# Attention scores of the first 128 tokens: one 32-bit matmul of 128 columns from plain queries and keys

## The chip, the core and the metric

The kernel runs on one core of one Trainium2 chip. Its time is the device time of one execution in microseconds (us); the time before is the median of three runs. Work runs on five engines, each with an instruction stream of its own: TensorE (PE in the profile; its weight loads are listed as PEld), VectorE (DVE), ScalarE (ACT), GpSimd (POOL) and SyncE (SP). They wait for each other through semaphores. TensorE writes to PSUM, eight banks of 128 x 512 32-bit numbers.

## The reference

One decoder layer over 512 tokens of width 1024, all in 32-bit floats. An input projection gives the parts of two mixers; a gated spatial mixer (A) and a sparse attention (B) are projected, gated and added, then follow an output projection and a feed-forward part. The attention, in the part that matters here:

```python
def block(i):                       # i = 0..3, blocks of 128 queries
    ...
    score = jnp.where(causal[None], score, -jnp.inf)
    sel_score, sel_idx = lax.top_k(score, top_k)       # top_k = 128
    valid = jnp.isfinite(sel_score)
    k_sel = gather(k, sel_idx).astype(jnp.float32)
    v_sel = gather(v, sel_idx).astype(jnp.float32)
    ...
    att = jnp.einsum('btgrd,btkgd->btgrk', qg.astype(jnp.float32), k_sel) * (HEAD_DIM ** -0.5)
    att = jnp.where(valid[:, :, None, None, :], att, NEG_INF)
    p = jax.nn.softmax(att, axis=-1)
    o = jnp.einsum('btgrk,btkgd->btgrd', p, v_sel).astype(q.dtype)
```

There are 8 query heads and 2 key heads, all of 128 dimensions. The first block has 128 causal keys at most and selects up to 128, so its queries attend to all their causal keys.

## The kernel before

**Split matmuls.** Most products take operands that are split into two parts of a reduced 32-bit type (`F32R`): hi is a copy in that type, lo is what is left. The helper `split` (line 359) makes hi with a ScalarE copy (line 360) and lo with a VectorE subtraction (line 361). `mm3` (line 51) then adds three matmuls into one PSUM tile: hi x hi (line 53), hi x lo (line 54) and lo x hi (line 55). Almost all matmuls of the kernel carry one of these three lines, so they are told apart by their tiles. Operands of the type `F32` go into a single `T.matmul` without a split; the token mixing of mixer A, `mix_mm` (line 914, matmul in line 918), is such a product.

**Order of work.** The order on each engine is that of the program text: the kernel is written out by hand, and the framework adds the waits between engines. Weights come through SP's queue into rotating buffers (`raw`), three of them. They are split ahead of use, hi by ScalarE (line 112) and lo by VectorE or GpSimd (line 116).

**Keys.** Early in the kernel, while the last queries are projected, `q_tasks` (line 800) runs small jobs ahead of each weight piece. Two of them are `k_b(0)` and `k_b(1)` (line 623): they split the rotated keys `kf` of one key head, 128 dimensions x 512 tokens, into `k_hi` and `k_lo`.

**Attention loop.** Line 1110 runs over 16 units of one block of 128 queries and one pair of heads (`aun`: block 3 first, block 0 last, four pairs each). Stage s issues: the value matmuls `at_pv` of unit s - 3; the scores `at_qk` (line 1013) of unit s; the sum with the mask and the row maximum, `at_soft_a` (VectorE, line 1033); the transposes `at_T` (line 1066) of unit s - 2 with their copies (ScalarE line 1123, VectorE line 1124); the normalization `at_soft_b` (line 1052) of unit s - 1; the exponential `at_exp` (ScalarE, line 1043) of unit s; the query split `at_split` (line 975) of unit s + 2; and a share of the gate projection as filler, `gb_part`. `at_qk` gives the queries to `mm3` as weights and the keys as the moving operand, for each of two heads. The number of columns is that of the causal keys, and at least 256.

**Buffers.** The rotated queries `qf` of two heads occupy the four buffers X0 to X3. Behind the loop these are taken over by the residual input, which the POOL queue loads again (`xr`, line 1138), each as soon as its buffer's last reader is done. The last reader of each is the unit of block 0 of that pair.

**Behind the loop.** The projection of mixer B (`W_PB`, the tiles `pb<-yb`) and then the output projection, which adds the residual.

Of the kernel before, what the change touches and what calls it, by code (L numbers as in the profile page):

```python
# [9 lines left out]
F32 = mybir.dt.float32  # L10
F32R = mybir.dt.float32r
I32 = mybir.dt.int32
AF = mybir.ActivationFunctionType
# [15 lines left out]
def block_kernel(ctx: ExitStack, tc: tile.TileContext, x, positions, w_ada, b_ada, w_in,  # L29
# [3 lines left out]
    T, V, A, P, SY = nc.tensor, nc.vector, nc.scalar, nc.gpsimd, nc.sync  # L33
# [8 lines left out]
    def bank(k, name="bank"):  # L42
        return psum.tile([128, 512], F32, name=name, tag=f"b{k}", bufs=1)

    def f(ap):
        return ap.bitcast(F32)
# [4 lines left out]
    def mm3(o, wl, rl, start, stop, **kw):  # L51
        (wh, wlo), (rh, rlo) = wl, rl
        T.matmul(o, wh, rh, start=start, stop=False, **kw)  # L53
        T.matmul(o, wh, rlo, start=False, stop=False, **kw)  # L54
        T.matmul(o, wlo, rh, start=False, stop=stop, **kw)  # L55
# [104 lines left out]
    mid = mid_stack.enter_context(tc.tile_pool(name="mid", bufs=1))  # L160
# [198 lines left out]
    def split(hi, lo, src):  # L359
        A.activation(hi, src, AF.Copy)  # L360
        V.tensor_sub(lo, src, f(hi))
# [217 lines left out]
    def rope_a(key, v, kind, m, t0=0):  # L579
        sh = t512("sh")[:m, t0:]  # L580
        V.stream_shuffle(sh, v, SW16 if kind == "q" else SW8)
        V.tensor_mul(sh, sh, tab[kind][:m, 1, t0:])
        V.tensor_mul(v, v, tab[kind][:m, 0, t0:])
        rp[key] = (v, sh)
# [6 lines left out]
    kf = mid.tile([128, 2, S], F32, name="kf", tag="A0", bufs=1)  # L591
# [3 lines left out]
    qf = [base.tile([128, 2, S], F32, name=f"qf{g}", tag=f"X{g}", bufs=1) for g in range(4)]  # L595
# [21 lines left out]
    k_hi = mid.tile([128, 2, S], F32R, name="k_hi", tag="k_hi", bufs=1)  # L617
    k_lo = mid.tile([128, 2, S], F32R, name="k_lo", tag="k_lo", bufs=1)

    def k_a(h):  # L620
        rope_a(("k", h), kf[:32, h], "q", 32)

    def k_b(h):
        split(k_hi[:, h], k_lo[:, h], kf[:, h])

    v_hi = mid.tile([128, 4, 256], F32R, name="v_hi", tag="v_hi", bufs=1)
    v_lo = mid.tile([128, 4, 256], F32R, name="v_lo", tag="v_lo", bufs=1)
# [157 lines left out]
    def q_rope(m):  # L785
        rope_a(("q", m), qf[m // 2][:32, m % 2], "q", 32)

    qstep = [0, 0]
    QT = {0: [lambda: q_rope(0), lambda: k_a(0)],
          1: [lambda: k_a(1), lambda: rope_b(("q", 0)), lambda: rope_b(("k", 0))],  # L790
          2: [lambda: rope_b(("k", 1)), lambda: qi_a(0)],
          3: [lambda: qi_b(0, 1), lambda: qi_a(1), lambda: qi_b(0, 0)],
          4: [lambda: qi_b(1, 1), lambda: qi_a(2), lambda: qi_b(1, 0)],
          5: [lambda: qi_b(2, 1), lambda: qi_a(3), lambda: qi_b(2, 0)],
          6: [lambda: qi_b(3, 1), lambda: qi_b(3, 0)],
          7: [ki_stats, lambda: k_b(0), ki_norm],
          8: [lambda: k_b(1)],
          10: [lambda: q_rope(1)]}

# [138 lines left out]
    def au_tasks():  # L938
        s = austep[0]
        austep[0] += 1  # L940
        if s == 0:
            for tk in range(4):
                ln_v(tk)
            rstd(rva, mva[:, :, 1], 4, 1.0)
            run_bg(0.8)
        elif s == 1:
            ln_v2(0)
            ln_v2(1)
        elif s == 2:
            ln_v2(2)  # L950
            ln_v2(3)
        for m in AT.get(s - 1, []):
            mix_ev(m)
        if s > 2:
            run_bg(1.6 if s < 8 else 2.0)
        if s in (20, 21):
            at_split(s - 20)
# [14 lines left out]
    AS = {}  # L972
    SCALE = 128 ** -0.5

    def at_split(u):
        i, hp = aun[u]
        qh = mid.tile([128, 2, 128], F32R, name="qh", tag="qh", bufs=2)
        ql = mid.tile([128, 2, 128], F32R, name="ql", tag="ql", bufs=2)
        split(qh, ql, qf[hp][:, :, i * 128:(i + 1) * 128])
        AS["q", u] = (qh, ql)  # L980
# [31 lines left out]
    yb = [(S2B[m // 2][:, m % 2], S2B[4 + m // 2][:, m % 2]) for m in range(8)]  # L1012
    def at_qk(u):
        i, hp = aun[u]
        nn = max((i + 1) * 128, 256)
        qh, ql = AS["q", u]
        g = hp // 2
        for e in range(2):
            p = bank(2 + e, "qk")
            mm3(p[:, :nn], (qh[:, e], ql[:, e]), (k_hi[:, g, :nn], k_lo[:, g, :nn]), True, True)  # L1020
            AS["s", u, e] = p

# [87 lines left out]
    for s in range(NU + 3):  # L1110
        if s >= 3:
            yh, yl, pp = at_pv(s - 3)
            A.activation(yh, pp, AF.Copy)
            V.tensor_sub(yl, pp, f(yh))
        if s < NU:
            at_qk(s)
            at_soft_a(s)
            if s == 0:
                pa_last[0]()
                at_split(2)  # L1120
        if 2 <= s <= NU + 1:
            for o, ol, p in at_T(s - 2):
                A.activation(o, p, AF.Copy)
                V.tensor_sub(ol, p, f(o))
        if 1 <= s <= NU:
            at_soft_b(s - 1)
        if s < NU:
            at_exp(s)
        if 0 < s < NU - 2:
            at_split(s + 2)  # L1130
        gb_part(GBN[s], 2 if s else 1)
# [495 lines left out]
    for q in range(-2, NQ):  # L1627
        g, u = 2 + q // 2, q % 2
# [282 lines left out]
```

## Time and profile before

| | |
|---|---|
| median of 3 runs | 824.95 us (824.74 to 825.56) |
| the profiled execution, its own time | 825.28 us |
| its span in the profile | 823.4 us |
| score matmuls in the span | 96, in 16 units of 6 |
| of these, block 0 | 24, in the units that start at 367.18, 371.83, 376.48 and 380.56 us |
| attention loop on TensorE | 306.8 to about 391.8 us |

The profile records one execution. A row of the timeline has the start in us from the start of the span, the duration in us, the engine, the line of the program, the operation, what it writes and reads (out<-in), its shape and how many are merged; in brackets stands how long the engine was idle before and what ended that. Matmuls overlap in the array, so a matmul's duration is longer than its share of TensorE's time, which is the distance from its start to the next one's. In rows of grouped instructions of one tile, three numbers behind the count are the shortest, median and longest duration in ns, and then come the first and last start. Waits are listed as who waited for whom, with us in total, times and the longest.

### The profile page before, as it was taken

The numbers are of one execution on the slowest core, as the hardware profiler recorded it, in microseconds if no ns is written. First come the engines' busy times: TensorE is split into PE (matmuls) and PEld (weight loads), VectorE is DVE, ScalarE is ACT, GpSimd is POOL, SyncE is SP. The second block draws the span as 40 slices with busy tenths as digits, with TensorE's granted clock in tenths as the row PEclk, the third lists the DMA queues.
The fourth block names the chain that finished last, engine by engine and source line by source line (L and its number), as shares of the span: only waits on it lengthen the run. The fifth ranks groups of instructions, "written<-read, shape, count | busy, mean of one in ns | idle before, by whom it ended". The sixth has DMA issues, their size and how long they took to land.

```text
span 823.4 us, 12920 instructions
## 1 busy us (share of the span) xinstructions
PE 808.5 (98%) x4920; PEld 722.0 (88%) x4920; DVE 684.9 (83%) x1167; ACT 427.7 (52%) x760; POOL 156.5 (19%) x171
## 2 busy tenths in 40 slices
PE   7999999999999999999999999999999999999996
PEld 6889889988888888988888899999999999888785
DVE  7989788798899558887688879889989888798676
ACT  6674444323332226665636586555555556666543
POOL 3060031362354411000000010222212222000001
PEclk9999999999999999999999999999999999999998
DMA  9974352332346553046630504889988978766543
GB/s 293 311 211 119 103 179 78 107 100 91 112 136 199 185 174 102 26 153 209 198 132 12 194 27 138 200 263 244 288 221 237 213 220 185 226 203 205 180 128 128
DMA packets 107197, 138.46 MB, mean 168 GB/s; under 512 B 6480, under 2 KB 77136, under 8 KB 106976
## 3 DMA queue, kind: packets, MB, share of 16 engines
q1 hardware_dynamic: 96832, 109.76, 42.8%
q0 software_dynamic: 9584, 27.07, 14.1%
q8 instruction: 38, 0.62, 0.3%
q10 hardware_dynamic: 720, 0.82, 0.3%
q14 instruction: 23, 0.19, 0.1%
HBM read 135.26 MB, written 23.07 MB: 192 GB/s over the span
## 4 chain that ended last, share of the span: by engine, by line
PE 51%; DVE 19%; DMA 5%; ACT 2%; issue 2%; POOL 0%; POOLq 0%; ACTq 0%; DVEq 0%
PE R L53 6%; PE R L54 6%; PE R L55 6%; DMA mraw<-in_w_ada_dram 5%; PE pfo L55 3%; PE pfo L54 3%; PE pfo L53 3%; DVE acc L177 3%; DVE sco L717 2%; DVE m L713 2%; PE pb L53 2%; PE pb L55 2%; PE pb L54 2%; DVE lo L116 2%; PE po L54 2%
## 5 line engine op out<-in xcount | busy, mean ns | idle before, releaser
L112 ACT ACTIVATE hi<-raw 128x1024 fp32r<-128x1024 f32 (+2 forms) x103 | 107.0, 1040 | 106.0 <-PE pb L54 35.7
L116 DVE TENSOR_TENSOR lo<-raw,hi 128x1024 fp32r<-128x1024 f32 (+2 forms) x67 | 81.1, 1214 | 29.4 <-ACT hi L112 28.9
L116 POOL TENSOR_TENSOR lo<-raw,hi 128x1024 fp32r<-128x1024 f32 x29 | 73.0, 2521 | 128.1 <-ACT hi L112 122.4
L53 PE MATMUL pb<-h,hi 128*128 128x512 f32 (+1 forms) x192 | 74.6, 388 | 0.0
L55 PE MATMUL pb<-h,lo 128*128 128x512 f32 (+1 forms) x192 | 73.9, 385 | 0.0
L54 PE MATMUL pb<-h,hi 128*128 128x512 f32 (+1 forms) x192 | 73.9, 385 | 0.0
L54 PE MATMUL pfo<-lo,za 128*128 128x512 f32 (+1 forms) x146 | 56.4, 386 | 0.3 <-DVE lo L116 0.3
L55 PE MATMUL pfo<-hi,za 128*128 128x512 f32 (+1 forms) x146 | 56.2, 385 | 0.0
L53 PE MATMUL pfo<-hi,za 128*128 128x512 f32 (+1 forms) x146 | 56.2, 385 | 0.0
L177 DVE SCALAR_TENSOR_TENSOR acc<-mraw,cols,acc 128x512 f32<-128x512 f32 x49 | 39.8, 813 | 19.6 <-DMA mraw<-in_w_ada_dram 18.6
L1239 POOL TENSOR_TENSOR sm<-sm,mhalf 128x1 f32<-128x1 f32 x8 | 5.3, 660 | 216.9 <-DVE sm L1238 216.9
L53 PE MATMUL R<-tb,sx 128*128 128x256 f32 x160 | 45.3, 283 | 1.1 <-ACT R L1661 0.7
L54 PE MATMUL R<-tb,sx 128*128 128x256 f32 x160 | 45.1, 282 | 0.0
L55 PE MATMUL R<-tb,sx 128*128 128x256 f32 x160 | 45.0, 281 | 0.0
L55 PE MATMUL R<-tb,lo 128*128 128x256 f32 x160 | 44.8, 280 | 0.0
L53 PE MATMUL R<-tb,hi 128*128 128x256 f32 x160 | 44.8, 280 | 0.0
L54 PE MATMUL R<-tb,hi 128*128 128x256 f32 x160 | 44.6, 279 | 0.0
L55 PEld LDWEIGHTS pb<-h,lo 128*128 128x128 f32 x192 | 36.0, 188 | 7.3
L54 PEld LDWEIGHTS pb<-h,hi 128*128 128x128 f32 x192 | 36.0, 188 | 6.9
L53 PEld LDWEIGHTS pb<-h,hi 128*128 128x128 f32 x192 | 36.0, 188 | 6.9
L324 POOL COPY sm<-sm 128x1 f32<-128x1 f32 x30 | 18.9, 631 | 117.0 <-ACT sm L323 116.9
L54 PE MATMUL pav<-lo,h 128*128 128x256 f32 x128 | 35.8, 279 | 0.0
(377 smaller groups left out, 2675.4 us busy)
## 6 DMA issues: line engine op xcount, KB each, us to landing
raw<-in_w_ffn_in_dram SPq DMA_DIRECT2D x44, 512.0 KB, 5.8
raw<-in_w_in_dram SPq DMA_DIRECT2D x40, 512.0 KB, 3.8
wsum<-in_w_ffn_out_dram POOLq DMA_DIRECT2D x30, 512.0 KB, 7.0
mraw<-in_w_ada_dram SPq DMA_DIRECT2D x28, 512.0 KB, 4.1
raw<-wsum SPq DMA_DIRECT2D x20, 512.0 KB, 3.9
raw<-in_w_ffn_out_dram SPq DMA_DIRECT2D x18, 512.0 KB, 4.5
s<-in_w_ada_dram SPq DMA_DIRECT2D x30, 256.0 KB, 5.6
wsum<-wsum POOLq DMA_DIRECT2D x10, 512.0 KB, 5.9
```

The source lines that it names most:

```text
L53: T.matmul(o, wh, rh, start=start, stop=False, **kw)
L54: T.matmul(o, wh, rlo, start=False, stop=False, **kw)
L55: T.matmul(o, wlo, rh, start=False, stop=stop, **kw)
L112: A.activation(hi[:, :m], e["raw"][:, :m], AF.Copy)
L116: e["lo"].tensor_sub(lo[:, :m], e["raw"][:, :m], f(hi[:, :m]))
L177: V.scalar_tensor_tensor(o, w, cs[:, j:j + 1], o, op0=OP.mult, op1=OP.add)
L324: P.tensor_copy(t, t)
L713: V.max(m8s[i], sco[i])
L717: V.match_replace(out=sco[i], in_to_replace=m8s[i], in_values=sco[i], imm_value=TAKEN)
L1239: P.tensor_tensor(r2[:, tk:tk + 1], r2[:, tk:tk + 1], mhalf[:, :1], op=OP.pow)
```

## The change

The units of block 0 no longer split their queries. Each of their heads has one matmul of two `F32` operands: the plain queries `qf` as weights and, as the moving operand, a plain copy of the first 128 keys, `k_pl`. This copy is made by ScalarE behind the split of the keys, one instruction for each key head. The other blocks keep their matmuls; the least number of 256 columns applied to block 0 alone and is gone with it.

```diff
@@ -617,11 +617,14 @@
     k_hi = mid.tile([128, 2, S], F32R, name="k_hi", tag="k_hi", bufs=1)
     k_lo = mid.tile([128, 2, S], F32R, name="k_lo", tag="k_lo", bufs=1)
 
+    k_pl = mid.tile([128, 2, 128], F32, name="k_pl")
+
     def k_a(h):
         rope_a(("k", h), kf[:32, h], "q", 32)
 
     def k_b(h):
         split(k_hi[:, h], k_lo[:, h], kf[:, h])
+        A.activation(k_pl[:, h], kf[:, h, :128], AF.Copy)
...
@@ -974,6 +977,8 @@
 
     def at_split(u):
         i, hp = aun[u]
+        if i == 0:
+            return
         qh = mid.tile([128, 2, 128], F32R, name="qh", tag="qh", bufs=2)
...
@@ -1012,11 +1017,15 @@
     def at_qk(u):
         i, hp = aun[u]
-        nn = max((i + 1) * 128, 256)
-        qh, ql = AS["q", u]
+        nn = (i + 1) * 128
         g = hp // 2
         for e in range(2):
             p = bank(2 + e, "qk")
+            if i == 0:
+                T.matmul(p[:, :nn], qf[hp][:, e, :nn], k_pl[:, g], start=True, stop=True)
+                AS["s", u, e] = p
+                continue
+            qh, ql = AS["q", u]
             mm3(p[:, :nn], (qh[:, e], ql[:, e]), (k_hi[:, g, :nn], k_lo[:, g, :nn]), True, True)
             AS["s", u, e] = p
```

## The prediction

> **What bounds the kernel now.** I read the page first, then the waits of TensorE over the whole span, then the timeline around the instructions that the change touches. All times are from one execution: 825.28 us, of which the profile's span holds 823.4 us. The median of the three runs is 824.95 us, so the profiled execution lies 0.33 us above it. Differences are worked out in the profile, and then taken off the median.
>
> ```profile
> span 823.4 us, 12920 instructions
> ...
> PE 808.5 (98%) x4920; PEld 722.0 (88%) x4920; DVE 684.9 (83%) x1167; ACT 427.7 (52%) x760; POOL 156.5 (19%) x171
> ...
> PEclk9999999999999999999999999999999999999998
> ```
>
> TensorE (PE) is busy for 98% of the span, with the full clock granted in every slice but a piece of the last. A busy share is modelled, so it alone doesn't prove the bound. The waits of TensorE do more, in us in total, times, longest:
>
> ```profile
> PE warm L502 <- DMA cst<-in_consts_dram: 5.3, 1, 5.3
> PE R L53 <- ACT R L1661: 0.7, 1, 0.7
> ...
> PE pv L54 <- DVE tl L1124: 0.2, 1, 0.2
> ```
>
> After the first load, no wait of TensorE is longer than 0.7 us, and the only one inside attention is 0.2 us. So in the attention loop the end is set by what TensorE itself has to stream, and other engines matter only if they become late for it.
>
> **The score matmuls that go.** The change touches the last four units of the loop, those of token block 0 (i = 0). The timeline of TensorE (start, duration, instruction) for the first, the second and the last of the four:
>
> ```profile
> 367.18 0.28 PE L53 MATMUL qk<-k_hi,qh 128*128 128x256 f32 x1
> ...
> 367.89 0.60 PE L1066 MATMUL pT<-cst,pt 128*128 128x128 f32 x4
> ```
>
> ```profile
> 371.83 0.28 PE L53 MATMUL qk<-k_hi,qh 128*128 128x256 f32 x1
> 371.95 0.28 PE L54 MATMUL qk<-k_lo,qh 128*128 128x256 f32 x1
> ...
> 372.42 0.28 PE L55 MATMUL qk<-k_hi,ql 128*128 128x256 f32 x1
> 372.54 0.60 PE L1066 MATMUL pT<-cst,pt 128*128 128x128 f32 x4
> ```
>
> ```profile
> 380.56 0.28 PE L53 MATMUL qk<-k_hi,qh 128*128 128x256 f32 x1
> ...
> 381.26 0.38 PE L1066 MATMUL pT<-cst,pt 128*128 128x128 f32 x2
> ```
>
> The 0.28 is the latency of one; what counts is the distance between starts, 0.12 us (371.83 to 371.95). A unit has two heads of three such matmuls, and occupies TensorE from its first score matmul to the first transpose: 0.71, 0.71 and 0.70 us here. Four units are 2.83 us, or 24 matmuls of 0.118 us. The two transposes behind them are not changed.
>
> **The matmuls that come.** Eight plain 32-bit matmuls, weights 128x128 (the queries) and 128 moving columns (the keys). The kernel has the same form elsewhere: the token mixing of the gated branch, line 918, has a plain 32-bit 128x128 as weights and 128 plain columns moving.
>
> ```profile
> L918 PEld LDWEIGHTS mix<-wmT,vg x64: 187/192/192, 187.1 to 227.9; 128*128 128x128 f32 x64
> L918 PE MATMUL mix<-wmT,vg x64: 270/275/275, 187.4 to 228.0; 128*128 128x128 f32 x64
> ```
>
> ```profile
> 187.15 0.39 PE L55 MATMUL pb<-h,lo 128*128 128x512 f32 x1
> 187.38 1.05 PE L918 MATMUL mix<-wmT,vg 128*128 128x128 f32 x8
> 188.19 0.48 PE L53 MATMUL pb<-h,hi 128*128 128x512 f32 x1
> 188.50 0.39 PE L54 MATMUL pb<-h,hi 128*128 128x512 f32 x1
> ```
>
> The loop over m and n issues 8 x 4 = 32 matmuls, and the trace has 64 records: each plain matmul is two instructions, with two weight loads. Four matmuls are the eight records from 187.38 to 188.19. The split matmul behind them is 0.31 us from its successor (188.19 to 188.50), where its kind takes 0.23 (187.15 to 187.38); those 0.08 belong to the plain group's end. So four cost 0.81 + 0.08 = 0.89 us, one costs 0.222, one record 0.111. The step from split to plain work shows no cost of its own: the split matmul ahead keeps its 0.23. In the changed loop the new matmuls are followed by the transposes, which are 128-column 32-bit work too, and the step back to split work stays where it is now. Eight cost 8 x 0.222 = 1.78 us.
>
> The saving on TensorE is 2.83 - 1.78 = **1.05 us**. No record of exactly these operands exists. From below, a record could stream its 128 columns at the rate of the split form, half of 0.118 = 0.059 us: 16 x 0.059 = 0.94, saving 1.89. From above, its weight load could stand in the open: 0.19 + 0.111 = 0.30 each, 4.82 in all, a loss of 1.99. I take 0.111, since line 918 agrees in shape, type and weight load.
>
> A rule speaks against the change: the Trainium skill, "FP8 and Floating Point Precision", section "TensorE Precision Notes", says that true 32-bit work takes four passes through the array, where the split form has three matmuls; it gives no price of a pass at 128 columns. Line 918 agrees with that if a pass costs half a record, 0.222 / 4 = 0.056 us, and then the sum stays 1.05; at a split matmul's 0.118 a pass, the change would lose, as the third rival below does.
>
> **What else is removed.** Four splits of the queries, each one ScalarE copy and one VectorE subtraction:
>
> ```profile
> L360 ACT ACTIVATE qh<-qf x16: 398/404/418, 279.9 to 375.3; 128x256 fp32r<-128x256 f32 x16
> L361 DVE TENSOR_TENSOR ql<-qf,qh x16: 415/420/426, 291.0 to 375.7; 128x256 fp32r<-128x256 f32 x16
> ```
>
> ScalarE loses 4 x 0.404 = 1.6 us and VectorE 4 x 0.420 = 1.7 us, two units ahead of the use. TensorE waits for neither, so I count nothing; the loop's one wait, 0.2 us, is in an earlier unit. These cuts also keep the softmax in step with the faster units. A unit's scores are normalized (line 1052) a stage before its transposes, and its transposed remainders (line 1124) come ahead of the value matmuls:
>
> ```profile
> 374.35 0.68 DVE L1124 TENSOR_TENSOR tl<-pT,th 128x512 fp32r<-128x512 f32 x1
> ...
> 375.14 0.48 DVE L1052 TENSOR_SCALAR pt<-pt,mx 128x128 f32<-128x128 f32 x2
> ...
> 375.78 0.19 PEld L54 LDWEIGHTS pv<-tl,v_hi 128*128 128x128 f32 x1
> ...
> 377.19 0.38 PE L1066 MATMUL pT<-cst,pt 128*128 128x128 f32 x2
> ```
>
> Normalized at 375.62, transposed at 377.19: 1.6 us of slack. Remainders at 375.03, loaded as weights at 375.78: 0.75 us. A unit gets 0.26 us shorter (1.05 / 4), so both hold.
>
> **What is added outside the loop.** Two ScalarE copies of keys, 128x128, behind the two splits of the keys near 90 us. Nearest row: a ScalarE pass of that shape in the loop takes 0.394 us; so at most 0.8 us for both, at least half the 128x256 split's 0.404 each, 0.4. The place:
>
> ```profile
> L1043 ACT ACTIVATE pt<-pt,mx 128x128 f32<-128x128 f32 x8 | 3.1, 394 | 1.5 <-DVE mx L1035 1.5
> ```
>
> ```profile
> 90.12 0.72 ACT L360 ACTIVATE k_hi<-kf 128x512 fp32r<-128x512 f32 x1
> 90.64 1.13 ACT L112 ACTIVATE hi<-raw 128x1024 fp32r<-128x1024 f32 x1
> ...
> 91.59 0.70 ACT L360 ACTIVATE k_hi<-kf 128x512 fp32r<-128x512 f32 x1
> ...
> 92.50 1.41 DVE L652 TENSOR_TENSOR v_lo<-pv,v_hi 128x256 fp32r<-128x256 f32 x4
> ...
> 93.83 1.22 DVE L116 TENSOR_TENSOR lo<-raw,hi 128x1024 fp32r<-128x1024 f32 x1
> 94.13 1.06 ACT L112 ACTIVATE hi<-raw 128x1024 fp32r<-128x1024 f32 x1 [1.85 <-issue]
> ```
>
> The first copy pushes the weight split at 90.64 by up to 0.4 us, to end at 92.2 instead of 91.8. Its remainder on VectorE starts at 93.83, behind v_lo, so 1.6 us of VectorE work covers it. The second falls into the 1.85 us in which ScalarE is idle. Cost nothing; with that cover gone, up to 0.8 us. It can't gain.
>
> **What moves.** The buffers of the queries become those of the reloaded residual (xr, line 1138, on the POOL queue). Their last reader was the split; now it is the score matmul, two units later.
>
> ```profile
> 361.99 0.62 POOL L1138 DMA_DIRECT2D xr<-in_x_dram  x1 [37.35 <-DVE ql L361]
> ...
> 376.41 0.53 POOL L1138 DMA_DIRECT2D xr<-in_x_dram  x1 [4.69 <-DVE ql L361]
> ```
>
> ```profile
> xr<-in_x_dram POOLq DMA_DIRECT2D x4, 512.0 KB, 3.6
> ```
>
> The first goes out near 367.7 instead of 361.99, and the last near 380.4 instead of 376.41 (ends of the units' matmuls, less the gain): four loads some 4 to 6 us late. POOL issues nothing else in that stretch, and the residual is wanted only by the output projection. They now run beside the loads of the next stage's weights, of which the second piece is the nearer:
>
> ```profile
> 386.52 1.22 DVE L116 TENSOR_TENSOR lo<-raw,hi 128x1024 fp32r<-128x1024 f32 x1
> ```
>
> ```profile
> 391.83 0.39 PE L53 MATMUL pb<-yb,hi 128*128 128x512 f32 x1
> ```
>
> Its split ends at 387.74, and TensorE uses it behind 24 matmuls of the first, at 391.83 + 24 x 0.23 = 397.4: 9.6 us of slack. Cost nothing.
>
> **Sum.** 825.28 - 1.05 = 824.23 us in the profiled execution's terms, **823.9 us** against the median.
>
> **The rivals.**
> *Cheaper records or shorter late waits (faster).* With 0.059 us a record the time is 824.95 - 1.89 = 823.1. A shift of phase could also shorten the late wait on R (0.7 us), giving 824.95 - 1.05 - 0.7 = 823.2. Line 918 speaks against the first, its wait on ScalarE's own chain against the second.
> *The gain is absorbed.* TensorE arrives earlier and waits for the softmax or for a load: 824.95. Against it, the slacks of 0.75, 1.6 and 9.6 us; for it, that 0.75 is small.
> *Four instructions a matmul.* Were the new matmul four instructions of 0.118 us instead of the two of line 918, 8 x 4 x 0.118 - 2.83 = +0.95: 825.9, slower by less than can be told. Against it, the 64 records for 32 matmuls; for it, nothing in the trace. The four passes that the Trainium skill names (page and section above) would be read so.
> *Weight loads in the open (slower).* The queries' plain weights can't be loaded under the matmul ahead. It decides from 2.83 / 16 = 0.177 us a record; at 0.30 it is +1.99, 826.9. Line 918 loads in 0.192 and still has 0.111 a record.
> *The moved loads delay the next weights (slower).* It decides once a weight load is more than 9.6 us late; with all four ahead of it, 4 x 3.6 = 14.4, TensorE waits 4.8: 824.95 - 1.05 + 4.8 = 828.7.
>
> **How the numbers follow.** What a measurement can tell from no change is about 0.2%, 1.65 us: from 823.3 to 826.6. Forecast 56%, cheaper records or late waits 18%, absorbed 10%, four instructions 3%, open weight loads 8%, moved loads 5%. Faster by over 0.2% is the second, 18%; slower the last two, 13%; within it the other three, 69%. The range of 822.9 to 825.4 holds the forecast, the absorbed case and most of the faster one; it leaves out the slower ones, 16%, and a little of the faster.
>
> **What would show it.** Sixteen records of scores from plain queries in the last four units, each unit 0.44 us from first score matmul to first transpose instead of 0.71; twelve query splits instead of sixteen; two copies near 91 us with no new wait of TensorE; the residual's loads released by TensorE. I am wrong if the records stand 0.15 us apart or more, or if a new wait of TensorE appears between 367 and 400 us.

## The result and the profile after

| | before | after |
|---|---|---|
| median | 825.16 us (824.59 to 826.51, 22 runs) | 823.93 us (822.93 to 826.04, 22 runs) |
| profiled span | 823.4 us | 822.3 us |

The ratio is 0.9987, with a 95% interval of 0.9981 to 0.9993: faster by 0.13%, or 1.1 us (0.6 to 1.6). The forecast was 823.9, a gain of 1.05. That 823.9 and 823.93 agree so closely is luck: the forecast starts from the 824.95 us of three runs, where 22 runs gave 825.16.

The page of the changed kernel:

```profile
span 822.3 us, 12898 instructions
...
PE 807.8 (98%) x4912; PEld 721.2 (88%) x4912; DVE 683.2 (83%) x1163; ACT 427.6 (52%) x758; POOL 156.3 (19%) x171
```

Eight matmul records fewer (24 go, 16 come), four VectorE instructions fewer, and two ScalarE instructions fewer (four go, two come). The new matmuls and what is left of the query split, in the view of their tiles:

```profile
L1025 PEld LDWEIGHTS qk<-k_pl,qf x16: 188/192/192, 366.9 to 379.8; 128*128 128x128 f32 x16
L1025 PE MATMUL qk<-k_pl,qf x16: 272/275/275, 367.0 to 380.0; 128*128 128x128 f32 x16
```

```profile
L360 ACT ACTIVATE qh<-qf x12: 398/406/417, 279.8 to 356.0; 128x256 fp32r<-128x256 f32 x12
```

TensorE in the first and the last unit of block 0:

```profile
367.01 0.61 PE L1025 MATMUL qk<-k_pl,qf 128*128 128x128 f32 x4
367.45 0.60 PE L1075 MATMUL pT<-cst,pt 128*128 128x128 f32 x4
...
379.62 0.61 PE L1025 MATMUL qk<-k_pl,qf 128*128 128x128 f32 x4
380.07 0.38 PE L1075 MATMUL pT<-cst,pt 128*128 128x128 f32 x2
```

A unit takes 0.44 us from its first score matmul to its first transpose (367.01 to 367.45; 0.45 in the last unit), where it took 0.71. One measure serves for all kernels below, the **block-0 stretch**: from the first score matmul of the first of the four units to the first transpose in the last. It contains the filler work too, which is the same in all of them. Before, it is 381.26 - 367.18 = 14.08 us, and after, 380.07 - 367.01 = 13.06: 1.02 us less. The changed kernel enters the stretch 0.17 us earlier and leaves it 1.19 us earlier; its span is 1.1 us shorter. So in these two executions the saving comes from the stretch and arrives at the end.

The waits of TensorE over the span:

```profile
PE warm L502 <- DMA cst<-in_consts_dram: 4.9, 1, 4.9
PE pfo L54 <- DVE lo L116: 1.0, 3, 0.4
PE modS L475 <- DVE accw L177: 0.4, 1, 0.4
PE R L53 <- ACT R L1683: 0.3, 1, 0.3
PE pfo L55 <- DVE gs L1795: 0.3, 1, 0.3
```

There is no wait in the loop. Behind it, the 0.7 us wait on R is gone and the waits on split weights have grown from 0.3 to 1.0 us: in these two executions late waits have moved, and they cancel. The last experiments return to that.

The two copies of keys on ScalarE, with the weight split behind the first and its remainder on VectorE:

```profile
90.48 0.38 ACT L627 ACTIVATE k_pl<-kf 128x128 f32<-128x128 f32 x1
90.68 1.13 ACT L112 ACTIVATE hi<-raw 128x1024 fp32r<-128x1024 f32 x1
...
92.15 0.38 ACT L627 ACTIVATE k_pl<-kf 128x128 f32<-128x128 f32 x1
...
93.67 1.22 DVE L116 TENSOR_TENSOR lo<-raw,hi 128x1024 fp32r<-128x1024 f32 x1
```

All of this run is 0.16 us earlier here; against that, the split starts 0.2 us late (90.68 for 90.64) and its remainder not at all (93.67 for 93.83).

The loads of the residual, on POOL's queue and in the list of DMA issues (median time to landing at the end):

```profile
367.92 0.62 POOL L1147 DMA_DIRECT2D xr<-in_x_dram  x1 [43.46 <-PE qk L1025]
...
380.53 0.53 POOL L1147 DMA_DIRECT2D xr<-in_x_dram  x1 [3.29 <-PE pT L1075]
```

```profile
xr<-in_x_dram POOLq DMA_DIRECT2D x4, 512.0 KB, 6.2
```

They are released by TensorE now, 4 to 6 us later, and land in 6.2 us instead of 3.6.

### The profile page after: what moved, and what is told of

It reads as the page before. It is cut to its first block, busy times and chain, and to the rows that moved or that the text cites. A ratio compares the mean times of both kernels' runs of the same rounds, so it can differ in the third digit from the quotient of the medians.

```text
span 822.3 us, 12898 instructions
## 1 busy us (share of the span) xinstructions
PE 807.8 (98%) x4912; PEld 721.2 (88%) x4912; DVE 683.2 (83%) x1163; ACT 427.6 (52%) x758; POOL 156.3 (19%) x171
## 4 chain that ended last, share of the span: by engine, by line
PE 53%; DVE 17%; DMA 5%; ACT 2%; issue 2%; POOL 0%; POOLq 0%; DVEq 0%; ACTq 0%
PE R L53 8%; PE R L54 8%; PE R L55 8%; DMA mraw<-in_w_ada_dram 4%; DVE acc L177 3%; PE pfo L55 3%; PE pfo L54 3%; PE pfo L53 3%; DVE lo L116 2%; DVE sco L720 2%; DVE m L716 2%; PE pb L53 2%; PE pb L55 2%; PE pb L54 2%; PE po L54 2%
```

## The experiments

Times in the table are of runs beside the kernel before, on the same chip. Where only one run was timed, its time is beside one run of before; such pairs scatter by more than the effects here, and what counts in them is the profile. Of block 1's units, those of the kernel before are 15.83 us by the same measure.

| kernel | median, us | of before, us | ratio, 95% interval | block-0 stretch, us |
|---|---|---|---|---|
| the change again | 823.55 | 824.81 | 0.9982 (0.9973 to 0.9991) | 13.06 |
| splits kept | 824.35 | 824.81 | 0.9993 (0.9983 to 1.0004) | 13.06 |
| split form, 128 columns | 824.89 | 824.81 | 1.0001 (0.9992 to 1.0011) | 13.81 |
| plain form, 256 columns | 824.71 | 824.81 | 0.9999 (0.9991 to 1.0008) | 14.73 |
| copies of keys alone | 824.84 | 824.51 | 0.9997 (0.9987 to 1.0007) | 14.09 |
| block 1 plain too | 823.51 | 824.51 | 0.9986 (0.9977 to 0.9994) | 13.06 |
| residual loaded late | 824.25 | 824.51 | 0.9991 (0.9980 to 1.0003) | 13.06 |
| split form, 192 columns | 826.16 (one run) | 825.49 | | 13.86 |
| plain form, twice 64 columns | 825.47 (one run) | 825.49 | | 14.67 |
| before, once more | 824.36 (one run) | 825.49 | | 14.09 |
| half weights added | 827.19 (one run) | 824.65 | | not compared |

The stretch of the same loop repeats within 0.01 us (14.08, 14.09, 14.09 for the three kernels with the old one; 13.06 five times for those with the new one), while the 95% intervals of the times in the table are 1.4 to 1.9 us wide. So questions of 0.1 to 1 us are decided by the stretch.

**Is it TensorE's stream? The change again, and with the splits kept.** The first has no edit.

> The changed kernel as it is, beside the kernel before on the same chip. Theory (TensorE's stream in the attention loop sets the time): units of block 0 take 0.44 us from first score matmul to first transpose instead of 0.71, 1.03 us less in all, so about 824.0 against 825.1. Rival (late waits of TensorE between 600 and 820 us carry part of the difference): the late waits, 3.0 us in all in both profiles seen so far, come out shorter than before by 0.3 us or more in this profile too.

The stretch is 13.06 us again, and the time is about 1.5 us (0.7 to 2.2) under before. The late waits of TensorE came out shorter as well, by the 0.3 us or more that the rival asks for: 2.4 us for 3.0 (counted as told under the last experiment). So this run alone doesn't settle where the time was gained; the kernel before, once more, bears on it.

The second makes the four query splits of block 0 that nobody reads:

```diff
     def at_split(u):
         i, hp = aun[u]
-        if i == 0:
-            return
         qh = mid.tile([128, 2, 128], F32R, name="qh", tag="qh", bufs=2)
```

> The changed kernel that still makes the four query splits of block 0 on ScalarE and VectorE, which nobody reads. Theory (TensorE's stream alone): the time of the change, 824.0, units still 0.44 us. Rival (part of the gain is the 1.6 us of ScalarE and 1.7 us of VectorE that the change removes): between the change and before, 824.5 or more, and a wait of TensorE in the loop.

Its profile, the tile of the split queries, the waits behind the loop and two rows of TensorE's timeline:

```profile
L360 ACT ACTIVATE qh<-qf x16: 398/404/417, 280.2 to 374.7; 128x256 fp32r<-128x256 f32 x16
```

```profile
PE R L53 <- ACT R L1668: 0.9, 1, 0.9
```

```profile
366.91 0.61 PE L1023 MATMUL qk<-k_pl,qf 128*128 128x128 f32 x4
...
379.97 0.38 PE L1073 MATMUL pT<-cst,pt 128*128 128x128 f32 x2
```

All sixteen splits are there again, and the stretch is still 13.06 us, with no wait in the loop. Removing the splits is worth nothing there. The time lies between the change and before, as the rival said, but its interval holds both; the profile has a late wait on R of 0.9 us, which the kernel before shows in one of two profiles (0.7 us; below). The time alone can't tell; the stretch does.

**Type or columns? The split form with 128 columns.**

```diff
-        nn = max((i + 1) * 128, 256)
+        nn = (i + 1) * 128
```

> The kernel before, with block 0's split matmuls cut from 256 columns to 128; no plain operands. Theory (the plain form is what makes 128 columns pay): a split matmul of 128 columns costs no less than one of 256, 0.118 us, so the time is that of before or more; if it costs as much as a plain matmul of 128 columns, 0.222 us, the four units take 24 x 0.222 = 5.33 us instead of 2.83, +2.5 us. Rival (only the columns count): 24 x 0.059 = 1.42 us, so -1.4 us against before, better than the change.

```profile
366.85 0.22 PE L53 MATMUL qk<-k_hi,qh 128*128 128x128 f32 x1
366.91 0.27 PE L54 MATMUL qk<-k_lo,qh 128*128 128x128 f32 x1
367.02 0.28 PE L55 MATMUL qk<-k_hi,ql 128*128 128x128 f32 x1
...
367.47 0.62 PE L1066 MATMUL pT<-cst,pt 128*128 128x128 f32 x4
```

Neither expectation holds. Half the columns save 0.09 us a unit (0.62 for 0.71), and 0.27 in the stretch, since the first transpose of each unit is now followed after 0.13 us instead of 0.11. The row distances tell why: the first matmul of the unit is followed after 0.06 us, each later one after 0.11. The stream alone would allow 0.06. Something else holds the later ones at 0.11, about what a plain record of 128 columns takes.

**What holds them? The split form with 192 columns, the plain form in two halves, and half weights.** The first has `nn = max((i + 1) * 128, 192)`.

> The kernel before with block 0's split matmuls at 192 columns instead of 256 (the last 64 belong to keys that aren't used). At 128 columns a unit was only 0.06 us shorter than at 256, 0.108 us a record. Theory (no record with its own weight load comes in less than about 0.11 us, and more columns cost once they exceed that): 192 columns cost 0.108 to 0.112 us a record, so a unit takes 0.65 to 0.67 us instead of 0.71. Rival (under 256 columns the split type streams at half its rate): 192 columns cost 1.5 times the 0.108 of 128, 0.16 us, so a unit takes 0.97 us.

```profile
368.37 0.25 PE L53 MATMUL qk<-k_hi,qh 128*128 128x192 f32 x1
368.46 0.27 PE L54 MATMUL qk<-k_lo,qh 128*128 128x192 f32 x1
368.57 0.28 PE L55 MATMUL qk<-k_hi,ql 128*128 128x192 f32 x1
...
369.02 0.60 PE L1066 MATMUL pT<-cst,pt 128*128 128x128 f32 x4
```

0.65 us: 0.09 for the first, 0.11 for the others. There is no slower stream under 256 columns, but a least distance. (The unit of 128 columns was 0.09 us shorter than that of 256, and not 0.06 as the expectation has it.) The plain form has it too:

```diff
-                T.matmul(p[:, :nn], qf[hp][:, e, :nn], k_pl[:, g], start=True, stop=True)
+                for c in (0, 64):
+                    T.matmul(p[:, c:c + 64], qf[hp][:, e, :nn], k_pl[:, g, c:c + 64], start=True, stop=True)
```

> The changed kernel with each plain matmul cut into two of 64 columns: the same products, twice the records and weight loads. Theory (about 0.11 us is also the least that a plain record takes): 8 records a unit of 0.108 to 0.111, 0.86 to 0.89 us instead of 0.44, +1.7 us in the four units. Rival (a plain record costs its columns alone, with 256 columns at 0.219 and 128 at 0.111): 0.055 us a record, a unit 0.44 us as in the change.

```profile
366.74 1.00 PE L1026 MATMUL qk<-k_pl,qf 128*128 128x64 f32 x8
367.58 0.61 PE L1076 MATMUL pT<-cst,pt 128*128 128x128 f32 x4
```

Eight records in 0.84 us: behind the first, which is followed after 0.06, they stand 0.11 apart. But for the first, half the columns don't shorten them. The last of the three adds to the split form of 128 columns, in each unit, 12 matmuls with weights of 64 queries, whose results nobody reads:

```diff
-        nn = max((i + 1) * 128, 256)
+        nn = (i + 1) * 128
...
             mm3(p[:, :nn], (qh[:, e], ql[:, e]), (k_hi[:, g, :nn], k_lo[:, g, :nn]), True, True)
+            for r in (0, 64) if i == 0 else ():
+                mm3(p[:64, 128 + 2 * r:256 + 2 * r], (qh[:, e, r:r + 64], ql[:, e, r:r + 64]),
+                    (k_hi[:, g, :nn], k_lo[:, g, :nn]), True, True)
```

> The kernel before with block 0's split matmuls at 128 columns (a unit of 0.62 us), and with 12 more split matmuls in each unit whose results nobody reads: the same products with weights of 64 queries instead of 128, 128 columns each. Theory (the least of 0.11 us a record is the load of 128 weight columns): with half the weights a record takes its stream, 0.058 us, so a unit takes about 0.62 + 12 x 0.058 = 1.3 us. Rival (it is a fixed price of an instruction): 12 x 0.11, a unit of 1.9 to 1.95 us.

```profile
366.98 0.19 PEld L53 LDWEIGHTS qk<-k_hi,qh 128*128 128x128 f32 x1
367.10 0.22 PE L53 MATMUL qk<-k_hi,qh 128*128 128x128 f32 x1
367.10 0.19 PEld L54 LDWEIGHTS qk<-k_lo,qh 128*128 128x128 f32 x1
...
367.21 0.19 PEld L55 LDWEIGHTS qk<-k_hi,ql 128*128 128x128 f32 x1
...
367.32 0.14 PEld L53 LDWEIGHTS qk<-k_hi,qh 128*64 128x64 f32 x1
367.38 0.23 PE L53 MATMUL qk<-k_hi,qh 128*64 128x128 f32 x1
367.38 0.14 PEld L54 LDWEIGHTS qk<-k_lo,qh 128*64 128x64 f32 x1
...
368.44 0.62 PE L1069 MATMUL pT<-cst,pt 128*128 128x128 f32 x4
```

With 64 weight columns (128*64 in the rows) and the same 128 moving columns, matmuls follow each other after 0.06 us, and a unit takes 1.34 us: 0.62 + 12 x 0.06. It isn't a price of the instruction. The least distance is the weight load, as the rows of the loads (PEld) show: behind a load of 128 columns the next load starts 0.11 us later (367.10, 367.21, 367.32), behind one of 64 columns 0.06 (367.32, 367.38). So a load of 128 columns takes about 0.11 us, and one of 64 at most 0.06. The Trainium skill, "TensorE: Matmul & The Clock Gate", section "LDWEIGHTS (loading the stationary operand)", gives the number of weight columns divided by 1.2 in nanoseconds, an estimate of 107 for 128 and 53 for 64. The trace agrees in the distance between loads, 0.11 us and 0.06; the rows of the loads themselves last longer, 0.19 and 0.14.

**Where does the plain form stop paying? 256 columns, and block 1 too.** The first computes 256 columns from both heads' copies and uses the half that it needs:

```diff
-                T.matmul(p[:, :nn], qf[hp][:, e, :nn], k_pl[:, g], start=True, stop=True)
-                AS["s", u, e] = p
+                T.matmul(p[:, :256], qf[hp][:, e, :nn], k_pl.rearrange("p h n -> p (h n)"), start=True, stop=True)
+                AS["s", u, e] = p[:, g * 128:(g + 1) * 128]
```

> The changed kernel with 256 moving columns in block 0's plain matmuls (both key heads' copies side by side; the half that belongs to the other head is computed and not used). Theory (a plain record's cost is its stream of columns): two records of 0.222 us a matmul, 16 x 0.222 = 3.55 us for the four units, +1.77 against the change and +0.72 against before: about 825.8. Rival (its cost is the weight load, or a fixed price of an instruction): still 0.111 us a record, the time of the change, 824.0.

```profile
366.81 1.03 PE L1025 MATMUL qk<-k_pl,qf 128*128 128x256 f32 x4
367.67 0.60 PE L1075 MATMUL pT<-cst,pt 128*128 128x128 f32 x4
```

0.86 us a unit, 0.215 a record; the stretch is 0.65 us longer than before and 1.67 longer than in the change. So at 256 columns the stream is the bound, at 128 the stream and the weight load are about equal. The time, 0.9999 (0.9991 to 1.0008), allows from -0.7 to +0.7 us and so can't show the +0.65.

The other makes block 1 plain as well:

```diff
-    k_pl = mid.tile([128, 2, 128], F32, name="k_pl")
+    k_pl = mid.tile([128, 2, 256], F32, name="k_pl")
...
-        A.activation(k_pl[:, h], kf[:, h, :128], AF.Copy)
+        A.activation(k_pl[:, h], kf[:, h, :256], AF.Copy)
...
-    bst = mid.tile([128, 4, 24], F32, name="bst")
+    bst = mid.tile([128, 4, 24], F32, name="bst", tag="qh", bufs=2)
...
-        if i == 0:
+        if i <= 1:
             return
...
-            if i == 0:
-                T.matmul(p[:, :nn], qf[hp][:, e, :nn], k_pl[:, g], start=True, stop=True)
+            if i <= 1:
+                T.matmul(p[:, :nn], qf[hp][:, e, i * 128:nn], k_pl[:, g, :nn], start=True, stop=True)
```

> The changed kernel with plain scores for block 1 too (256 columns, which the split form doesn't pad); a small statistics tile shares a buffer to make room. Theory (a plain record costs its columns): block 1 has eight heads of two records of 0.222 us instead of three of 0.118, 8 x (0.444 - 0.354) = +0.72 us against the change: 824.7. Rival (saving records and splits pays whatever the columns): 16 records instead of 24 at 0.111 to 0.118 us, -1.0 us against the change: 823.0.

Block 1's units on TensorE, in this kernel and in the kernel before:

```profile
346.91 1.03 PE L1025 MATMUL qk<-k_pl,qf 128*128 128x256 f32 x4
...
363.39 0.60 PE L1075 MATMUL pT<-cst,pt 128*128 128x128 f32 x4
```

```profile
347.40 0.28 PE L53 MATMUL qk<-k_hi,qh 128*128 128x256 f32 x1
...
363.23 0.60 PE L1066 MATMUL pT<-cst,pt 128*128 128x128 f32 x4
```

16.48 us instead of 15.83: block 1 loses 0.65, close to the 0.72 worked out, and the rival's gain isn't there. The time, about 1.2 us (0.5 to 1.9) under before, doesn't show the loss. It is no better than the change's, whose 1.1 us lies inside; its profile happens to have 0.3 us of waits on split weights where the change's has 1.0. I don't count this as a better version.

**The parts outside the loop: the copies alone, and the residual loaded late.** The kernel before plus the copies, which nobody reads (`k_pl` and the copy in `k_b`, as in the diff of the change):

> The kernel before plus the two copies of keys, which nobody reads. Theory (they lie under other work near 91 us): the time of before, 825.1, no new wait of TensorE, and the remainder of the weights on VectorE still starts near 93.8 us. Rival (their cover is gone): up to +0.8 us, with a wait of TensorE between 90 and 105 us.

```profile
91.74 1.13 ACT L112 ACTIVATE hi<-raw 128x1024 fp32r<-128x1024 f32 x1
...
94.72 1.22 DVE L116 TENSOR_TENSOR lo<-raw,hi 128x1024 fp32r<-128x1024 f32 x1
```

This execution is 0.9 us late from its start on (its k_hi copy begins at 91.02, for 90.12), and the remainder at 94.72 is no later than that. TensorE has no wait between 80 and 450 us, so no cost of the copies shows.

The changed kernel with the residual's loads held until the gates are done:

```diff
+    A.activation(mva[:, 0, 0:1], gbt[3][:, 0, 0:1], AF.Copy)
+    P.tensor_copy(mva[:, 0, 0:1], mva[:, 0, 0:1])
     for i in range(4):
         xt[i] = base.tile([128, D], F32, name=f"xr{i}", tag=f"X{i}", bufs=1)
         P.dma_start(xt[i], x[i * 128:(i + 1) * 128, :])
```

> The changed kernel with all four loads of the residual held back until the gates behind the loop are done, some 16 to 29 us later than in the change, in one burst beside the next stage's weight loads. Theory (the residual is wanted much later, and the weights have 9.6 us of slack): the time of the change, 824.0, no wait of TensorE between 390 and 440 us. Rival (the loads crowd out the weights): up to 4.8 us more, with waits of TensorE on the split of weights there.

VectorE in this kernel, at the modulation sum and at a later weight split; then VectorE in the change at the same two instructions; then TensorE in this kernel:

```profile
409.51 1.54 DVE L177 SCALAR_TENSOR_TENSOR acc<-mraw,cols,acc 128x512 f32<-128x512 f32 x2 [2.05 <-DMA mraw<-in_w_ada_dram]
...
475.44 1.22 DVE L114 TENSOR_TENSOR wx<-raw,wx 128x1024 fp32r<-128x1024 f32 x1
```

```profile
406.19 1.53 DVE L177 SCALAR_TENSOR_TENSOR acc<-mraw,cols,acc 128x512 f32<-128x512 f32 x2
...
473.32 1.22 DVE L114 TENSOR_TENSOR wx<-raw,wx 128x1024 fp32r<-128x1024 f32 x1
```

```profile
482.78 0.28 PE L53 MATMUL pf<-h,wx 128*128 128x256 f32 x1
483.30 0.38 PE L54 MATMUL pf<-h,wx 128*128 128x256 f32 x1 [0.23 <-DVE h L1293]
```

Four loads in one burst from 398.3 us do crowd out others. The two pieces of weights issued among them take 8.1 and 7.2 us to land, where the change's take 3.5 and 4.9, and a piece of the modulation matrix (mraw) takes 6.9 instead of 3.7. The weights still come in time: ScalarE's copies of them wait for TensorE and not for the load. For mraw VectorE waits 2.05 us. At the stretch (first matmul at 367.96 for 367.01) this execution was already 0.95 us behind the change, from differences before it. VectorE is 3.3 us behind at the modulation sum and still 2.1 at the weight split. TensorE has no wait between 390 and 440 us, as the theory said, but in the first matmuls of the next part it meets the late VectorE: in the rows above two neighbours stand 0.52 us apart instead of 0.12, and two smaller gaps precede them. Over the three, TensorE goes from 0.96 to 1.94 us behind the change, a loss of 1.0. So the rival's mechanism exists: the weights were crowded out as it said, but the wait reached TensorE by another path, with loads some 20 to 30 us later than in the change. That the delay of 409 us is the one that TensorE meets at 483 is read from these rows, not tested. With the change's own 4 to 6 us, no such wait shows. The time, 0.9991 (0.9980 to 1.0003), lies between the change and before and decides nothing.

**Do the late waits belong to the change? The kernel before, once more.** No edit.

> The kernel before, unchanged, profiled once more. Theory (the late waits of TensorE differ from one execution to the next of the same kernel): the wait of 0.9 us near 617 us in the first profile is shorter or gone, or others between 600 and 820 us change by 0.3 us or more. Rival (they belong to the kernel): the same waits at the same places, within 0.1 us. The units of block 0 take 0.71 us with either.

Its waits of TensorE from 600 us on, all of them:

```profile
PE R L53 <- ACT R L1674: 0.3, 1, 0.3
PE pfo L54 <- DVE lo L116: 0.3, 1, 0.3
PE pfo L55 <- DVE gs L1786: 0.3, 1, 0.3
```

The same program, the same stretch (14.09), and the 0.7 us wait on R of the first profile (ACT R L1661) is gone. The change's second profile has 0.6 us on split weights where its first had 1.0. Counted from the distances between starts of matmuls from 600 us on, beyond the usual distance of their kind, TensorE loses 2.9 and 1.8 us in the two profiles of before, and 3.0 and 2.4 in the two of the change. So the rival of the first experiment is not borne out: the kernel before can have the shorter late waits as well. Late waits vary by about 1 us within a program, as much as the change saves. Whether a few tenths of them follow the change stays open: waits on split weights between 710 and 720 us, 0.7 and 0.3 us, stand in both profiles of the change and in neither of before, but the profiles with the splits kept and with block 1 plain, which have the new loop too, show none there. What sets them in an execution wasn't traced.

## Why the prediction was right, by its steps

**The bound.** That TensorE's own stream sets the end in the loop held: the stretch lost 1.02 us and the span 1.1, and removing or keeping the splits on the other engines made no difference to the stretch.

**The cost of the split matmuls, 2.83 us.** Held by both profiles of before, 0.71 us a unit. The reason for it was incomplete: I took the 0.118 us to be 256 columns of stream. That is true at 256, but 128 columns would not have halved it, because 128 weight columns take 0.11 us to load.

**The cost of the plain matmuls, 1.78 us.** Measured 1.77: 0.44 in the rows of three units and 0.45 in the last. Taking the form from line 918, same shape, type and weight load, was what made this term right, and with it the saving in the stretch, 1.02 us for 1.05.

**The bounds of that cost.** The lower one, 0.059 us a record, can't be held with 128 weight columns: the plain form cut in halves gave 0.11 behind its first record. The cheaper-record rival, part of the 18%, is thereby out. The upper one, 0.30, didn't come either: the loads of plain weights run under the matmuls ahead (16 loads of 0.19 us latency in units of 0.44 us). Four instructions a matmul is out too, with 16 records for 8 matmuls.

**What is removed from ScalarE and VectorE, counted as nothing.** Held: 13.06 us with the splits and without.

**The copies of keys, at most 0.8 us of ScalarE, counted as nothing.** They took 2 x 0.38, and with the copies alone no wait of TensorE arose between 80 and 450 us.

**The moved loads, counted as nothing.** Issued at 367.92 to 380.53, where I had said near 367.7 to 380.4. The term that was off is their duration: I used the 3.6 us of the kernel before, and issued among the weight loads they took 6.2. They slowed the weights too: the second piece of the next projection, which took 5.0 us to land, took 8.1. The slack covered both. The rival was right that moved loads delay the next weights and can cost TensorE time, wrong in where: with the loads held much longer, the first wait was VectorE's for the modulation matrix, and not one for the weights.

**The gain isn't absorbed.** The softmax slacks held: no wait of TensorE in the loop in either profile of the change. Late waits differ by more between executions of one kernel than between the kernels, so four profiles can't tell whether they absorb a part; over 22 runs each the gain is 1.1 us (0.6 to 1.6), which leaves room for about 0.4 of the 1.02.

## What to carry to other kernels

Before you narrow a matmul, ask for its weight load: with 128 weight columns loaded for each matmul, nothing under 0.11 us was to be had in a run of them, so 24 split matmuls of 128 columns were hardly cheaper than of 256, and 16 plain records were. The plain 32-bit form, two records a matmul, beats three split ones where the moving side is 128 columns wide, and loses at 256. When two executions differ by as much as the effect, compare a stretch that begins and ends on the same instructions: it repeated within 0.01 us where medians of 11 runs left intervals of 1.4 us or more.

## What the runs showed of the hardware

The split type at 128 and 192 columns streams in 0.06 and 0.09 us (the first matmul of a unit), in proportion to 0.12 at 256; there is no slower stream below 256 columns. The rival of the run with 192 columns was that there might be one.

The first short matmul behind longer ones is cheap, 0.06 us and not 0.11, in every unit of the split form with 128 columns. The rows of the run with half weights show it: the first short matmul starts 0.12 us after its weight load (366.98, 367.10), for that load ran under a matmul of 0.118 us, and a later one 0.06 after its own (367.32, 367.38). Behind long matmuls the weight loads are that much further ahead of the stream, and one short matmul uses it up.
